# One transformer layer on one core: attention values as two scaled fp16 halves, a fixed instruction order, and weight splits on GpSimd

## The chip, the cores and the metric

The kernel runs on 1 core of one Trainium2 chip, as one launch. The core has a matrix engine (TensorE, called PE in the profile, with its weight loads PEld), three elementwise engines (VectorE or DVE, ScalarE or ACT, GpSimd or POOL) and a queue engine (SyncE or SP) that here issues nearly all DMAs. Each engine works through its own list of instructions in order and waits at an instruction whose operands are not ready. The metric is the device time in microseconds (us), the median of the runs shown. PE works in its fp32 replacement type (fp32r, shown as f32 or fp32r), so products that must be exact to fp32 are made of three: high half by high half, and the two crossed ones.

## The reference, cut to what matters

One layer maps 1024 latent tokens (width 1024) and 256 context tokens to 1024 latent tokens: a modulated norm, one wide input projection, two mixers side by side (attention and a bidirectional mLSTM), a gated merge, then a gated feed-forward net. The change touches the attention and what is drawn from the same activations `h` beside it:

```python
q = apply_rope(rms_norm(heads(aq, 16, 64), q_norm_w), cos, sin)
k = apply_rope(rms_norm(heads(ak, 4, 64), k_norm_w), cos, sin);  v = heads(av, 4, 64)
# per block of 128 queries: keys of the blocks b-1, b, b+1 with |i-j| <= 128, and all 256 context keys
s = concat(where(valid, q k^T, -1e30), q k_ctx^T) * 64 ** -0.5
p = softmax(concat(s, sink))                    # sink: one learned logit per head
att = p[lat] v + p[ctx] v_ctx                   # 16 query heads share 4 key/value heads
y = (sigmoid(ga) * (att w_branch_att) + sigmoid(gm) * (ml w_branch_ml)) w_out
```

`ga` and `gm` are projections of the same `h`; the kernel computes these two while it is in the attention.

## The kernel before, in words

The program runs in stages: startup (modulation, norms, context projections, and the latent activations turned into `hH`, `hL`, the two halves of `h`), attention, mLSTM, and the tail (merge and feed-forward net). The change leaves the mLSTM and the tail as they are.

**Rounds.** `stage_attention` walks through 4 groups g (one key/value head and its four query heads) of 8 blocks b of 128 tokens: 32 blocks. Round n works on four blocks at once: it projects block n (`proj`, 24 matmuls of 384 columns into `pq`; `projected` then makes norms, rotary products and values), turns block n-1 into key and query layout (`stacks`: transposes `qt`, halves `QT`, `KA`, `KB`), computes the scores of block n-3 for four heads (`scores`), and the weighted values of block n-4 (`pv`). Between these lies `filler`: one tile of `ga` or `gm`, 24 matmuls of 512 columns, 32 tiles in all.

**One head of scores** (`head`, lines 677 to 694): four matmuls into a bank `s` (there are two such banks); a fused DVE pass adds the mask, scales and takes the running extreme (L683); ACT makes the shift (L688), the probabilities as fp16 `P` (L691) and again in fp32 over `s` with their sum (L692); DVE makes the low half, fp32 minus fp16 (L693), and a DMA transpose on SP turns both halves into `T` (L694). `P` has three buffers, `T` two.

**Values.** `V` holds a value head as two fp32r halves. [...] `end` adds the two halves of the result, multiplies by the turned reciprocal sum `R`, which goes through DRAM (`norm_row`), and stores.

**Weights.** Projection and gate weights come as fp32 through a pool of two raw buffers and are split into halves by ACT (the copy, L46) and DVE (the rest, L76 and L51). `mod_product` sums a row of later modulation weights, one or two DVE passes a round over the one buffer `wmb` (L234, L236).

**Order.** The program is written as a recipe; a scheduler lays every engine's list out from it by its own estimates. `issue_after` pins a few instructions behind others.

## Time and profile before

| what | value |
|---|---|
| median of 3 runs | 1930.26 us (1928.48 to 1932.29) |
| the profiled execution, its own time | 1935.92 us |
| its span, first to last instruction | 1934.1 us |
| PE busy in the span | 1847.9 us |
| DVE, ACT, POOL busy | 1446.8, 1031.2, 432.2 us |
| first attention projection on PE | 102.5 us |
| first score matmul | 130.7 us |
| first mLSTM matmul | 667.9 us |

The profile is of one execution. Times are microseconds from the first instruction. A group row names the line of the kernel, the engine, the operation, what it writes and reads, its shape and count; then busy time in us and mean duration in ns; then the engine's idle time just before these instructions and what ended it. A timeline row has start, duration, engine, line and tiles; in square brackets stands the idle time before it and what ended that. Matmuls overlap in the pipeline, so what one costs in a stream is the distance between starts, which is shorter than the duration shown.

### The profile page before, as it was taken

What the parts mean: (1) busy time and instruction counts of PE and PEld (TensorE: products, weight loads), DVE (VectorE), ACT (ScalarE), POOL (GpSimd) and SP (SyncE); (2) the same over time, 40 slices, a digit from 0 to 9 for tenths busy, and PEclk for the clock granted to TensorE, in tenths of its full rate; (3) what the DMA queues carried; (4) which work ended last, traced back from release to release, by engine and by line L of the source; (5) the groups of instructions that cost most, each with busy time, mean ns of one, the idle gap of its engine ahead of it and who ended that gap; (6) DMA issues with size and microseconds to landing.
All of it is one profiled execution on the core that took longest, in us unless ns stands there. A gap on an engine that the chain in (4) does not pass through costs nothing.

```text
span 1934.1 us, 27646 instructions
## 1 busy us (share of the span) xinstructions
PE 1847.9 (96%) x9061; PEld 1558.6 (81%) x9061; DVE 1446.8 (75%) x2864; ACT 1031.2 (53%) x2110; POOL 432.2 (22%) x733
## 2 busy tenths in 40 slices
PE   7899889989988899999999999999999999999999
PEld 4877777777777698988888888888888888888887
DVE  3857667878676568586758778769989888897565
ACT  4746666666666645354446556256545444455441
POOL 1225556555545623030211012010000000000000
PEclk9999999999999999999999999999999999999999
DMA  9547667767665942426235982822354544499851
GB/s 359 163 135 169 140 129 156 164 149 178 134 156 113 201 139 82 167 78 223 85 117 186 379 322 87 288 88 78 140 200 181 196 153 176 162 326 346 299 171 66
DMA packets 301984, 342.46 MB, mean 177 GB/s; under 512 B 175872, under 2 KB 200464, under 8 KB 299024
## 3 DMA queue, kind: packets, MB, share of 16 engines
q1 hardware_dynamic: 287440, 314.47, 53.4%
q10 hardware_dynamic: 14400, 26.22, 4.2%
q8 instruction: 72, 1.18, 0.3%
q14 instruction: 72, 0.59, 0.1%
HBM read 224.61 MB, written 76.16 MB: 156 GB/s over the span
## 4 chain that ended last, share of the span: by engine, by line
PE 63%; DVE 10%; DMA 7%; ACT 7%; POOL 7%; issue 5%; ACTq 0%; SPq 0%; POOLq 0%; DVEq 0%
PE pa L1682 4%; PE pa L1684 4%; PE pa L1683 4%; PE g L758 3%; PE yb L1682 2%; PE yb L1683 2%; PE yb L1684 2%; PE dx L1684 2%; PE dx L1682 2%; PE dx L1683 2%; PE pb L1682 2%; PE pb L1684 2%; PE pb L1683 2%; DMA T<-P 2%; ACT s L692 2%
## 5 line engine op out<-in xcount | busy, mean ns | idle before, releaser
L683 DVE CUSTOM_DVE_ANT_0 s<-s,maskA,nsink 128x640 f32<-128x640 f32 (+1 forms) x128 | 115.9, 910 | 30.6 <-PE s L680 30.6
L693 DVE TENSOR_TENSOR P<-s,P 128x640 f16<-128x640 f32 (+1 forms) x128 | 100.7, 787 | 43.9 <-ACT s L692 43.4
L718 POOL CAST ph<-T 128x512 fp32r<-128x512 f16 x152 | 98.6, 649 | 115.8 <-DMA T<-P 73.2
L758 PE MATMUL g<-hH,fh 128*128 128x512 f32 x256 | 105.7, 413 | 4.8 <-ACT fo L46 3.4
L758 PE MATMUL g<-hH,fl 128*128 128x512 f32 x256 | 104.6, 409 | 0.0
L758 PE MATMUL g<-hL,fh 128*128 128x512 f32 x256 | 104.1, 407 | 0.0
L691 ACT ACTIVATE P<-s,st 128x640 f16<-128x640 f32 (+1 forms) x128 | 97.9, 765 | 3.2 <-ACT st L688 0.2
L718 POOL CAST pl<-T 128x512 fp32r<-128x512 f16 x152 | 96.4, 634 | 0.0
L692 ACT ACTIVATE s<-s,st 128x640 f32<-128x640 f32 (+1 forms) x128 | 94.0, 734 | 0.0
L585 PE MATMUL pq<-w1h,hH 128*128 128x384 f32 (+1 forms) x256 | 88.7, 347 | 3.3 <-ACT w1h L46 2.1
L585 PE MATMUL pq<-w1h,hL 128*128 128x384 f32 (+1 forms) x256 | 91.3, 357 | 0.0
L585 PE MATMUL pq<-w1l,hH 128*128 128x384 f32 (+1 forms) x256 | 88.5, 346 | 2.0 <-DVE w1l L76 2.0
L1096 POOL TENSOR_SCALAR kwh<-k,gcall 128x128 fp32r<-128x128 f32 x72 | 33.7, 472 | 232.5 <-PE dC L99 148.2
L677 PE MATMUL s<-KA,QT 128*128 128x384 f32 (+1 forms) x128 | 45.9, 358 | 31.2 <-DVE P L693 13.6
L98 PE MATMUL kv<-w1h,hH 128*128 128x384 f32 x208 | 71.6, 344 | 2.1 <-DVE VL L51 1.9
L1820 ACT ACTIVATE cv<-ua,vecT 128x1024 f32<-128x1024 f32 x22 | 27.4, 1244 | 84.6 <-DVE ua L1793 84.6
L99 PE MATMUL kv<-w1l,hH 128*128 128x384 f32 x208 | 70.5, 339 | 0.0
L100 PE MATMUL kv<-w1h,hL 128*128 128x384 f32 x208 | 70.3, 338 | 0.0
L1682 PE MATMUL dx<-dwh,dfh 128*128 128x512 f32 (+1 forms) x176 | 68.4, 388 | 0.0
L1684 PE MATMUL dx<-dwh,dfl 128*128 128x512 f32 (+1 forms) x176 | 68.3, 388 | 0.0
L1683 PE MATMUL dx<-dwl,dfh 128*128 128x512 f32 (+1 forms) x176 | 68.2, 387 | 0.0
L46 ACT ACTIVATE dfh<-drf 128x512 fp32r<-128x512 f32 x55 | 34.3, 628 | 58.5 <-PE dx L1683 26.4
(610 smaller groups left out, 6387.8 us busy)
## 6 DMA issues: line engine op xcount, KB each, us to landing
ur<-in_w_up SPq DMA_DIRECT2D x22, 1024.0 KB
wmb<-in_w_modB SPq DMA_DIRECT2D x48, 256.0 KB
f_d<-cv SPq DMA_DIRECT2D x22, 512.0 KB
wm<-in_w_modA SPq DMA_DIRECT2D x16, 512.0 KB
fr<-in_w_g SPq DMA_DIRECT2D x32, 256.0 KB
drf<-fs_d SPq DMA_DIRECT2D x15, 512.0 KB
drw<-wt_d SPq DMA_DIRECT2D x14, 512.0 KB
w1b<-in_w_cx SPq DMA_DIRECT2D x16, 388.0 KB
```

Source lines behind the costliest of these rows:

```text
L98: nc.tensor.matmul(ps, lh[:, ls], rh[:, rs], start=start and i == 0, stop=False)
L99: nc.tensor.matmul(ps, lh[:, ls], rl[:, rs], start=False, stop=False)
L585: return lambda: nc.tensor.matmul(ps[:, :wn], x, w[:, :wn], start=i == 0, stop=i == len(todo) - 1)
L683: nc.vector.tensor_tensor_reduce(e, e, mask, scale=ss[:, h : h + 1], scalar=nsink[:, hh : hh + 1], op0=ALU.add, op1=ALU.min, accum_out=st4 ...
L691: nc.scalar.activation(hi, e, AF.Exp, bias=m, scale=-1.0)
L692: nc.scalar.activation(e, e, AF.Exp, bias=m, scale=-1.0, accum_out=st4[:, 4 + h : 5 + h])
L693: nc.vector.tensor_tensor(lo, e, hi, op=ALU.subtract)
L718: nc.gpsimd.tensor_copy(x, T[:, i * nk + kb].rearrange("p h q -> p (h q)"))
L758: return lambda: nc.tensor.matmul(ps, w, x, start=i == 0, stop=i == len(todo) - 1)
L1682: nc.tensor.matmul(ps, lh, rh, start=start and i == 0, stop=False, skip_group_check=True)
L1683: nc.tensor.matmul(ps, lh, rl, start=False, stop=False, skip_group_check=True)
L1684: nc.tensor.matmul(ps, ll, rh, start=False, stop=stop and i == n - 1, skip_group_check=True)
```

## The change

**Values as fp16.** `V` (latent) and a new `Vx` (context, per group) are kept as two fp16 halves, scaled so that they fit: from the sum of squares of the group's value weights, the modulation and the context values a bound is made (`value_bound` once at startup, `value_squares` and `value_scale` once per group: ACT squares, one matmul by ones, two DVE passes, three small POOL passes), whose root is the factor `down` and whose inverse is `up`. `up` enters where `V` is written, `down` where the reciprocal sums are turned (`norm_row`). `T` then goes into the product as it is: the 304 casts and their buffers are gone, and each of the 304 value matmuls is fp16 by fp16.

**Order.** The loop stands under `manual_schedule`: each engine gets the attention's instructions in the order in which they are written, with every head, transpose, projection and gate piece put at a chosen place. The four blocks per round stay; there are 36 rounds where there were 37, and gate tile 0 is in round 0, tile j in round j+2. The low half of the fourth head, its transpose and the sum move to the start of the next round.

**GpSimd splits** the gate weights and, for groups 1 to 3, the projection weights (`gate_split`, `weight_split`: a cast and a subtraction each), loaded one to three rounds ahead. The query scale goes into the norm weight, so one small POOL pass per block is gone; the key's factor goes into the rotary products, and POOL writes the key twice, so one ACT pass (`kf`) is gone. The modulation rows get two buffers.

Around one block of the third group, PE's list had, before (`g`: gate tile, `s`: scores, `po`: weighted values; `Pool_49` is a wait for POOL):

```order
L758 MATMUL g9_1_4960<-hH4_90,fl9_1_4771 128x512
L722 MATMUL po2_2_4964<-ph2_2_0_4965,V2_3861 128x512 [waits Pool_49]
L722 MATMUL po2_2_4964<-pl2_2_0_4966,V2_3861 128x512 [waits Pool_49]
L722 MATMUL po2_2_4964<-ph2_2_1_4969,V2_3861 128x512 [waits Pool_49]
L722 MATMUL po2_2_4964<-pl2_2_1_4970,V2_3861 128x512 [waits Pool_49]
L677 MATMUL s2_3_3_5101<-KA2_3859,QT2_3_4652 128x384 [waits DVE_49,PE_49]
```

and now:

```order
L736 MATMUL s2_3_2_4794<-KcB_127,QT2_3_4413 128x256
L581 MATMUL g10_0_4780<-hH2_88,fl10_0_4401 128x512
L581 MATMUL g10_0_4780<-hH3_89,fh10_0_4400 128x512
L581 MATMUL g10_0_4780<-hL3_97,fh10_0_4400 128x512
L581 MATMUL g10_0_4780<-hH3_89,fl10_0_4401 128x512
L581 LDWEIGHTS V2_3683 [waits DMAHW7_49,DMAHW4_49,DMAHW2_49]
L581 MATMUL po2_2_4818<-T2_2_4528,V2_3683 128x512 [waits DMAHW0_49]
```

All value matmuls of a block now stand in one piece behind head 2's scores, and the wait for the four transposes (`DMAHW`), which POOL's first cast had, stands in PE's own list.

POOL's list around the same block had, before:

```order
L718 CAST ph2_2_2_4973<-T2_2_4779 128x512 [waits PE_49]
L718 CAST pl2_2_2_4974<-T2_2_4779 128x512 [waits PE_49]
L600 TENSOR_SCALAR ss2_6_5056<-ss2_6_5056 128x5 [waits DVE_49]
L718 CAST ph2_2_3_4977<-T2_2_4779 128x512 [waits PE_49]
L718 CAST pl2_2_3_4978<-T2_2_4779 128x512 [waits PE_49]
L718 CAST ph2_2_4_4981<-T2_2_4779 128x512 [waits PE_49]
L718 CAST pl2_2_4_4982<-T2_2_4779 128x512 [waits PE_49]
L601 TENSOR_TENSOR ss2_6_5056<-ss2_6_5056,expo_62 128x5 [waits Pool_49]
```

and now:

```order
L798 TENSOR_TENSOR o22_1_4664<-o22_1_4664,R17_4636 64x512 [waits DMAHW6_49,DMAHW3_49,DVE_49]
L571 CAST fh11_0_4745<-fr11_0_4698 128x512 [waits DMAHW5_49,PE_49]
L572 TENSOR_TENSOR fl11_0_4746<-fr11_0_4698,fh11_0_4745 128x512 [waits PE_49,Pool_49]
L571 CAST fh11_1_4749<-fr11_1_4700 128x512 [waits DMAHW6_49,PE_49]
L572 TENSOR_TENSOR fl11_1_4750<-fr11_1_4700,fh11_1_4749 128x512 [waits PE_49,Pool_49]
L639 TENSOR_SCALAR ss2_6_4829<-ss2_6_4829 128x5 [waits DVE_49]
L640 TENSOR_TENSOR ss2_6_4829<-ss2_6_4829,expo_62 128x5 [waits Pool_49]
L672 TENSOR_TENSOR qf2_6_4834<-qf2_6_4834,t22_6_4835 128x256 [waits DVE_49]
```

The block's norm factors `ss` and rotary sum `qf` no longer stand among casts that wait for PE to free a buffer; the gate weights' splits stand there instead, two rounds ahead of their use.

At the end of the startup SP's list had, before (`w1r`: first projection weights):

```order
L529 DMA vx_d_105<-kvx2_1_961 128x388 [waits DMAHW3_49,DVE_49]
L221 DMA wmb0_1113<-in_w_modB 128x512 [waits DMAHW4_49,PE_49]
L529 DMA vx_d_105<-kvx3_0_1073 128x372 [waits DMAHW5_49,DVE_49]
L529 DMA vx_d_105<-kvx3_1_1077 128x372 [waits DMAHW6_49,DVE_49]
L73 DMA w1r25_1128<-in_w_att0 128x800 [waits DMAHW7_49,DVE_49]
```

and now:

```order
L855 DMA wr0_1_1134<-in_w_att0 128x800 [waits DMAHW1_49]
L523 DMA vx_d_105<-kvx2_0_973 128x388 [waits DMAHW2_49,DVE_49]
L523 DMA vx_d_105<-kvx2_1_976 128x388 [waits DMAHW3_49,DVE_49]
L855 DMA wr0_2_1140<-in_w_att0 128x800 [waits DMAHW4_49,DVE_49,Activation_49]
L855 DMA wr0_3_1146<-in_w_att0 128x800 [waits DMAHW5_49,DMAHW1_49,DVE_49]
L564 DMA fr0_0_1152<-in_w_g 128x512 [waits DMAHW6_49,DMAHW4_49,DVE_49]
```

The four loads of the first projection weights have moved ahead of the gate's and, the first of them, by some dozen DMAs; before, they stood behind the store of the last context columns (`vx_d<-kvx3`).

The diff, cut to its core (the products, the splits, the scale and the loop):

```diff
-        nc.gpsimd.tensor_scalar(ss[:, :4], ss[:, :4], -(HD ** -0.5), 1.0, op0=ALU.mult, op1=ALU.mult)
-                nc.gpsimd.tensor_copy(x, T[:, i * nk + kb].rearrange("p h q -> p (h q)"))
-                split_from(nc, fh, fl, raw)
...
+    def weight_split(g, k2):
+        raw = RAW.pop(("w", g, k2))
+        h, lo = wts.halves(f"a{g}_{k2}", raw.shape[2])
+        nc.gpsimd.tensor_copy(h, raw)
+        nc.gpsimd.tensor_tensor(lo, raw, h.bitcast(F32), op=ALU.subtract)
...
+                V=kp.tile([P, NB, P], F16, tag="V", name=f"V{g}"),
+                Vx=kp.tile([P, NCB, P], F16, tag="Vx", name=f"Vx{g}"),
...
+    def value_scale(g, ps, q):
+        nc.tensor.matmul(ps[:, 448:453], at.ones, q, start=True, stop=True)
+        t = wp.tile([P, 4], F32, tag="vs", name=f"vs{g}")
+        nc.vector.tensor_reduce(t[:, 0:1], ps[:, 448:452], axis=AX.X, op=ALU.add)
+        nc.vector.scalar_tensor_tensor(t[:, 1:2], t[:, 0:1], at.bound, ps[:, 452:453], op0=ALU.mult, op1=ALU.add)
+        nc.gpsimd.tensor_scalar(t[:, 1:2], t[:, 1:2], 2.0 ** -30, 1e-30, op0=ALU.mult, op1=ALU.add)
+        nc.gpsimd.tensor_tensor(t[:, 2:3], t[:, 1:2], expo[:, 0:1], op=ALU.pow)
+        nc.gpsimd.tensor_tensor(t[:, 3:4], t[:, 1:2], t[:, 2:3], op=ALU.mult)
+        G[g]["up"], G[g]["down"] = t[:, 2:3], t[:, 3:4]
...
+        copy_act(nc, G[g]["V"][:, b, 0:HD], ps[:, 320:384], scale=G[g]["up"])
...
+            V[:, b, HD:P], ps[:, 320:384], G[g]["up"], V[:, b, 0:HD], op0=ALU.mult, op1=ALU.subtract
...
+        todo = [(V[kb], T[:, i * nk + kb].rearrange("p h q -> p (h q)")) for kb in range(nk) for i in range(2)]
...
+    TILES = {0: 0}
+    TILES.update({j + 2: j for j in range(1, 32)})
+    LAST = N + 4
...
+    with tc.manual_schedule():
+        for n in range(LAST):
...
+            if tile_done:
+                gate_act(*tile_done)
+            if prior:
+                prior.sink_exp()
+            if S:
+                S.product(0)
+                S.top(0)
+                S.exps(0)
+            if prior:
+                prior.low(3)
+                prior.total()
+            mod_sum()
+            ps, new = proj(*now) if now else (None, Products())
+            new.some(14)
+            pt = turn(*turned) if turned else (tp_tile(f"nr{n}") if prior else None)
+            if out_done:
+                pv_end(*out_done)
+            if n % 2 == 0 and 1 <= n // 2 < 16:
+                for i in range(2):
+                    gate_split(n // 2, i)
...
+            q = value_squares(g) if fresh else None
+            if S:
+                S.product(1)
+            if turned:
+                turned_act(*turned, pt)
+            if S:
+                S.top(1)
+                S.exps(1)
+                S.low(0)
+            new.some(len(new.todo))
+            if prior:
+                prior.norm_turn(pt[0:4, 384:512])
+            if fresh:
+                value_scale(g, ps, q)
...
+            gate.some(8)
+            if turned:
+                turned_dve(*turned, pt)
...
+            if S:
+                S.product(2)
+            gate.some(4)
+            sq = values_act(*now, ps) if now else None
+            if prior:
+                prior.norm_row(pt[0:4, 384:512])
+            if S:
+                S.top(2)
+                S.exps(2)
+                S.low(1)
...
+            po, old = pv(*valued) if valued else (None, Products())
+            old.some(10)
+            if now:
+                ss = values_dve(*now, ps, sq)
+                qf, t2 = rope_q(*now, ps)
...
+            if S:
+                S.product(3)
+            o2 = pv_act(*valued, po) if valued else None
+            gate.some(24)
...
+            if S:
+                S.top(3)
+                S.exps(3)
+                S.low(2)
+            if now:
+                rope_k(*now, ps, ss, qf, t2)
+            if valued:
+                nc.vector.tensor_tensor(o2, po[0:HD], o2, op=ALU.add)
+            if S:
+                S.sinks()
+            mod_end()
...
+            prior = S
```

More of the change, by code (lines that the diff above doesn't have):

```diff
@@ L618, in projected @@
-        nc.gpsimd.tensor_tensor(qf, qf, t2, op=ALU.add)
-        S1[(g, b)] = (qf, ss)
-    def norm_row(pt):
-        if not SUMS:
-            return
-        sums, j = SUMS.pop()
-        nc.tensor.transpose(pt, sums, ident)
-        row = wp.tile([4, P], F32, tag="row", name=f"row{j}", bufs=1)
-        copy_act(nc, row, pt)
-        nc.sync.dma_start(norm_d[j].rearrange("(h t) -> h t", h=4), row)
-        R[j] = wp.tile([HD, 512], F32, tag="R", name=f"R{j}", bufs=1)
-        nc.sync.dma_start(R[j], norm_d[j : j + 1].to_broadcast([HD, 512]))
@@ L634, in stacks, with turn @@
+    def turn(g, b):
         qf, ss = S1.pop((g, b))
-        kf = wp.tile([P, 2, HD], F32, tag="kf", name=f"kf{n}", bufs=1)
-        copy_act(nc, kf, qf[:, None, 256:320].to_broadcast([P, 2, HD]), scale=ss[:, 4:5])
-        pt = tp_tile(f"qt{n}")
-        for i in range(2):
+        pt = tp_tile(f"qt{g}_{b}")
+        for i in range(3):
             nc.tensor.transpose(pt[:, i * P : (i + 1) * P], qf[:, i * P : (i + 1) * P], ident)
-        nc.tensor.transpose(pt[:, 256:384], kf.rearrange("p r d -> p (r d)"), ident)
@@ L706, in scores, with norm_turn, norm_row, norm_load @@
-        return head, sums
+        def norm_turn(self, pt):
+            nc.tensor.transpose(pt, self.st4[:, 12:16], ident)
+        def norm_row(self, pt):
+            j = self.g * NB + self.b
+            row = wp.tile([4, P], F32, tag="row", name=f"row{j}", bufs=1)
+            copy_act(nc, row, pt, scale=G[self.g]["down"][0:4])
+            nc.sync.dma_start(norm_d[j].rearrange("(h t) -> h t", h=4), row)
+        def norm_load(self):
+            j = self.g * NB + self.b
+            R[(self.g, self.b)] = wp.tile([HD, 512], F32, tag="R", name=f"R{j}", bufs=1)
+            nc.sync.dma_start(R[(self.g, self.b)], norm_d[j : j + 1].to_broadcast([HD, 512]))
@@ L734, in pv @@
[L734 to L752 removed]
+        po = mm_tile(f"po{g}_{b}")
```

472 lines of the change are left out of this document (268 added, 204 removed).

## The prediction

> **What bounds the kernel now.** I read the page's head and engine sums first, then the 40 slices, then the windows view cut at the first score, the last full round and the first mLSTM matmul, with a piece of the mLSTM for comparison. The columns of a window are start:end, length, busy us and count of PE, PEld, DVE, ACT and POOL, granted clock, DMA share, GB/s.
>
> ```profile
> span 1934.1 us, 27646 instructions
> PE 1847.9 (96%) x9061; PEld 1558.6 (81%) x9061; DVE 1446.8 (75%) x2864; ACT 1031.2 (53%) x2110; POOL 432.2 (22%) x733
> PE   7899889989988899999999999999999999999999
> ```
>
> ```profile
> 130.70:600.00 469.30, 426.31 (x2131) 362.43 (x2130) 347.42 (x839) 304.26 (x755) 257.54 (x396) 0.97 0.68 149
> 600.00:669.70 69.70, 56.38 (x250) 45.09 (x249) 43.28 (x94) 45.49 (x106) 36.45 (x57) 0.91 0.73 160
> 1100.00:1500.00 400.00, 398.46 (x1779) 327.54 (x1778) 336.76 (x483) 213.26 (x351) 24.92 (x20) 1.00 0.50 179
> ```
>
> PE's share of 96% is a mean: slices 2 to 13 have gaps, all later ones are full. From 1100 to 1500 PE is busy 398.46 of 400 us; the order of instructions there is not touched, so whatever is won or lost must arise before 669.7 us and arrives whole at the end. The attention's 28 full rounds last 469.3 us, **16.76 us a round**, with 43 us of idle PE. That idle is not all: after it matmuls run at half pace.
>
> ```profile
> 400.17 0.34 PE L585 MATMUL pq<-w1l,hH 128*128 128x384 f32 x1
> 400.34 0.34 PE L585 MATMUL pq<-w1h,hL 128*128 128x384 f32 x1
> ...
> 403.79 0.36 PE L677 MATMUL s<-KA,QT 128*128 128x256 f32 x1 [1.92 <-DVE st L699]
> 403.99 0.28 PE L678 MATMUL s<-KB,QT 128*128 128x256 f32 x1
> 404.11 0.28 PE L679 MATMUL s<-KcA,QT 128*128 128x256 f32 x1
> ...
> 407.21 0.63 PE L758 MATMUL g<-hL,fh 128*128 128x512 f32 x1
> 407.64 0.63 PE L758 MATMUL g<-hH,fl 128*128 128x512 f32 x1
> ...
> 409.77 0.39 PE L758 MATMUL g<-hL,fh 128*128 128x512 f32 x1
> 410.00 0.39 PE L722 MATMUL po<-pl,Vc 128*128 128x512 f32 x1
> ```
>
> From start to start a 384-column matmul takes .173 us, a 256-column one .12, a 512-column one .23, but .43 some microseconds after the 1.92 us wait. A round's need at full pace is 24 × .1735 = 4.16 (projection), 24 × .2315 = 5.55 (gate), 4 × (2 × .174 + 2 × .117) = 2.32 (scores), 10 × .231 = 2.31 (values) and about .55 of transposes: **14.9 us**. The round loses 1.9 us to waits and to slow matmuls behind them. Who makes PE wait:
>
> ```profile
> POOL ph L718 <- DMA T<-P: 65.5, 21, 8.4
> PEld po L722 <- POOL ph L718: 13.2, 21, 2.0
> PE s L677 <- DVE st L699: 11.6, 11, 2.3
> PE s L677 <- DVE P L693: 9.4, 11, 2.4
> ```
>
> Two chains end last: casts on POOL before the value products, and DVE's list, where the pass that frees a score bank stands behind others.
>
> **The change part by part.** POOL, DVE and ACT first (the figure behind the first bar's comma is the mean of one, in ns).
>
> ```profile
> L718 POOL CAST ph<-T 128x512 fp32r<-128x512 f16 x128 | 82.4, 644 | 100.6 <-DMA T<-P 65.5 <-PE po L722 15.0 <-DMA norm_d<-row 5.7
> L728 POOL TENSOR_TENSOR o<-o,R 64x512 f32<-64x512 f32 x26 | 34.5, 1328 | 84.3 <-DVE st L700 49.9 <-DVE o L727 28.2 <-DVE P L693 4.9
> L683 DVE CUSTOM_DVE_ANT_0 s<-s,maskA,nsink 128x640 f32<-128x640 f32 x84 | 78.9, 944 | 17.2 <-PE s L680 17.2
> L693 DVE TENSOR_TENSOR P<-s,P 128x640 f16<-128x640 f32 x83 | 68.1, 821 | 25.9 <-ACT s L692 25.5
> L51 DVE TENSOR_TENSOR fl<-fr,fh 128x512 fp32r<-128x512 f32 x25 | 24.4, 975 | 1.9 <-ACT fh L46 1.9
> L76 DVE TENSOR_TENSOR w1l<-w1r,w1h 128x768 fp32r<-128x768 f32 x12 | 13.5, 1126 | 3.2 <-ACT w1h L46 3.2
> L691 ACT ACTIVATE P<-s,st 128x640 f16<-128x640 f32 x83 | 65.7, 791 | 1.9
> L692 ACT ACTIVATE s<-s,st 128x640 f32<-128x640 f32 x83 | 63.2, 761 | 0.0
> L688 ACT ACTIVATE st<-st,shift 128x1 f32<-128x1 f32 x111 | 32.2, 290 | 38.0 <-DVE st L683 34.5 <-DVE st L700 2.5
> ```
>
> *POOL* is busy 257.54 us in the 28 rounds, 9.2 a round; 164 of it are the casts (128 of each half, .64 each). What stays is 3.3 a round. It gains the splits: half a gate tile by a cast of .64 and a subtraction, which no row shows on POOL (nearest, L728, 1.33; bounds .64 and 2.0): 1.97 a round, and the weight split about 1.2. Its sum is 6.5 to 7.3 of 14.9 us, done rounds ahead of the use: hidden. Only the key's second rotary add, under .5 us, lies in the key's path.
>
> *DVE* is busy 347.42 / 28 = 12.4 us a round, and loses L51 and L76, 1.35 of it. Set end to end for a block with three key blocks, its groups' means make 14.2 a round before and **12.9** now. *ACT* loses the copies behind these splits and `kf` (all L46), 1.3 us: end to end from 12.85 to 11.5. Both now lie two microseconds or more below PE's 14.9.
>
> *The fixed order.* I laid one round by hand from these durations, time 0 at head 0's product on PE. PE comes to head 1 at 3.4, the gate at 5.8, head 2 at 7.7, the values at 9.2, head 3 at 11.5, the end at 14.9. Head 3's low half of the round before ends on DVE at 2.6, so head 1's bank is free .8 us early; head 0's low ends at 5.9 (needed 7.7), head 1's at 10.2 (needed 11.5). The projection's slot comes free .9 us early, when the rotary products have read it; the turn's inputs, two us early. Nothing on this sheet makes PE wait, and the smallest margin is .8 us. But the margins hang on DVE's list of 12.9 us running with little delay, so the full floor is unlikely.
>
> *Values without casts.* The wait for `T` moves into PE's list, ahead of the 10 value matmuls; behind it stand the rest of the gate and head 3's product, and all of DVE's and ACT's work on head 3 waits for that. A transpose after the low half:
>
> ```profile
> 402.97 0.68 DVE L693 TENSOR_TENSOR P<-s,P 128x512 f16<-128x512 f32 x1
> ...
> 407.31 0.61 POOL L718 CAST ph<-T 128x512 fp32r<-128x512 f16 x1 [3.65 <-DMA T<-P]
> ...
> 650.46 4.64 DMA T<-P
> 663.89 2.73 DMA T<-P
> ```
>
> Low half ended 403.65, first reader 407.31: 3.7 us. With low 3 at 2.6 `T` is there at 6.3 and wanted at 9.2: 2.9 us of slack, cost zero; at 4.64 + .8 of issue it still fits. No fp16 matmul stands in the trace; I take the .23 of the fp32r row of the same width, and a tenth either way is 304 × .023 = 7 us, which goes into the range. The Trainium skill, "TensorE: Matmul & The Clock Gate", section "Back-to-back issue gap", gives N/2.4 + 2.5 ns for an isolated gap, 216 ns at 512 columns, and 131 ns in a sustained stream. The row of before has 230 for fp32r; by the page 304 value matmuls would be 4 to 30 us shorter if fp16 runs so and fp32r does not. No run here shows it, so it is left out of the sum.
>
> *Start.* The first weights were loaded behind the stores of context columns.
>
> ```profile
> 93.51 0.60 PE L435 MATMUL xt<-ident,x 128*128 128x128 f32 x4
> 96.19 1.54 SPq L73 DMA_DIRECT2D w1r<-in_w_att  x2
> 102.51 0.45 PE L585 MATMUL pq<-w1h,hH 128*128 128x400 f32 x1 [2.05 <-ACT w1h L46]
> 130.68 0.28 PE L677 MATMUL s<-KA,QT 128*128 128x256 f32 x1
> ```
>
> The four loads, .77 us of issue each, move past a dozen others on SP, the context stores among them; these come 3 us later, and their reader, the first value product, is four rounds away: no cost. Loaded early, the weights are split when `x` is turned at 94. Then projection 4.3 → 98.3, gate tile 0 with the value scale 5.8 → 104.1, second projection 4.3 and a little → 108.8; the third round's turn waits for the norm chain of ACT, DVE and POOL passes, about 6.5 → 115.4; copies → first score at 116, taken as 117 (bounds 114, nothing waits; 122, the POOL chains of the scale are in the way) against 130.7: **−13.7**. Two gate tiles fewer are done by then; they lie in the rounds counted next.
>
> *End.* Before, 69.7 us from 600 to the point where only mLSTM is left. Now one full round, then round 32 (no projection, ACT-bound) 11, round 33 10.5, rounds 34 and 35 together 15: four heads on ACT 9.5, a low half .8, a transpose 2.7, eight value matmuls 1.9. Sum r + 36.5, with ±5 for the bare end.
>
> *The sum* for a round of r us: start −13.7; 28 rounds 28 r − 469.3, less 1 (edge blocks with two key blocks save 6.4, 400-wide projections and three rounds with a new group's scale, estimated at 1.5 each, cost 5.4); end r + 36.5 − 69.7. At the floor, r = 14.9: −85. At today's 16.76: −31. Break-even is r = 17.8. **I take r = 15.2**, near the floor because the sheet has no wait, .3 above it for collisions of DMAs and small delays on DVE: −13.7 − 44.7 − 18.0 = −76.4. The profiled execution takes 1935.92 us, 5.7 above the median; it would be 1859.5, the median 1930.26 − 76.4 = **1854 us**.
>
> **The rivals.** *A: DVE becomes the bound.* DVE passes with two operands in SBUF stretch while POOL works:
>
> ```profile
> 426.66 0.69 DVE L51 TENSOR_TENSOR fl<-fr,fh 128x512 fp32r<-128x512 f32 x1
> 432.61 1.28 POOL L728 TENSOR_TENSOR o<-o,R 64x512 f32<-64x512 f32 x1 [3.82 <-DVE st L700]
> 432.90 1.54 DVE L51 TENSOR_TENSOR fl<-fr,fh 128x512 fp32r<-128x512 f32 x1 [0.28 <-ACT fh L46]
> ```
>
> The same pass takes .69 with no wide POOL pass beside it and 1.54 beside L728, and ends .55 after L728 has ended. POOL's splits can do this to the 1.5 modulation passes a round (both operands in SBUF), each held for nearly a whole split of 1.97, say 1.8 us, in a list with .8 us of margin: DVE 12.9 + 2.7 = 15.6, r = 15.6, −65, about 1865. It decides once the holds add up to 2 us a round. Against it: most DVE passes read a PSUM bank, and POOL works 7.3 us at most where it worked 9.2 before. The Trainium skill, "SBUF — State Buffer", section "Who interferes with whom", calls this one shared port pair, taken as an exclusive lock. The two rows above agree.
>
> *B: the round stays as it is*, because a chain of four heads through PE, DVE, ACT and back to a bank, rather than casts, sets it: r = 16.76, −31, about 1899. For it: bank waits (L699, L693) are as long as the casts'. Against it: the sheet.
>
> *C, slower: PE stands at the value products.* PE has no fill ahead of `T` that it may take out of turn, so if `T` lands more than 6.6 us after low 3 (2.9 of slack over 3.7), the rest of the gate and head 3 are late by the excess, in every round; with slow matmuls after each idle, half as much again. Slower than before needs r above 17.8, 2.6 over forecast: a landing some 9 us after the low half, in nearly all rounds, against 8.4 as the longest single wait for `T` now, in which POOL's own early arrival is counted. At 18.2 it gives +12, about 1942.
>
> **How the numbers follow.** Forecast .62, A .18, B .11, C .06; other cases .03. The range reaches from 1836 (floor of 14.9, first score at 114, the end 5 shorter and a little) to 1890 (into B, r = 16.45); outside remain C, part of B and some of the rest, under .2. Faster than before is everything but C and half the rest; .2%, 3.9 us, is about what a measurement of this kernel tells from none: faster .92, same .02, slower .06.
>
> **What would show it.** Right: the first score at 114 to 122, round starts 15 to 15.5 us apart, next to no PE idle at the value products, a clock of 1.00 in the rounds, no casts of `T`, mLSTM beginning near 593. A shows as full DVE slices and modulation passes above 1.5 us; B as bank waits before score products of a microsecond or more; C as idle on the values' weight load, ended by `T`. The whole is wrong if PE's idle per round is not below .5 us, or if PE's later stages change their length.

## The result and the profile after

The changed kernel takes **1877.4 us** (median of 4 runs, 1875.2 to 1879.1) against 1931.3 (4 runs, 1928.5 to 1934.2): ratio 0.972, 95% interval 0.9702 to 0.9739. That is 54 us, 2.8%, where 76 were forecast. The two profiled executions differ by 58.0 us (1935.92 and 1877.91), since the profiled one of before lay 4.6 us above its median and that of now 0.5. The page's head, engine sums, PE's slices and the granted clock:

```profile
span 1876.1 us, 27488 instructions
PE 1820.5 (97%) x9071; PEld 1526.3 (81%) x9071; DVE 1415.1 (75%) x2828; ACT 1010.6 (54%) x2078; POOL 365.0 (19%) x549
PE   8989999999996999999999999999999999999999
PEclk9999999999997999999999999999999999999999
```

Of the attention's gaps two slices are left: the third (94 to 141 us, the start) and the thirteenth (563 to 610 us, the end). The windows view, cut at the first projection, the first score, the start of the last round with a projection (28 rounds later) and the first mLSTM matmul (columns as in the prediction):

```profile
90.91:116.61 25.70, 22.39 (x109) 19.95 (x108) 16.94 (x40) 9.48 (x27) 15.62 (x23) 0.94 0.47 138
116.61:542.10 425.49, 413.94 (x2208) 345.12 (x2207) 319.23 (x815) 289.94 (x728) 201.03 (x240) 1.00 0.79 168
542.10:610.12 68.02, 50.85 (x228) 36.55 (x228) 45.93 (x100) 41.48 (x97) 15.04 (x40) 0.84 0.83 186
1050.00:1450.00 400.00, 398.49 (x1779) 327.81 (x1778) 334.59 (x478) 208.60 (x340) 24.89 (x20) 1.00 0.49 176
```

The 28 rounds take 425.5 us in place of 469, **15.20 a round** against 15.2 in the sum, at a clock of 1.00 in place of 0.97. The first score is at 116.6 (forecast 117). But the end, from 542.1 to 610.1, takes 68.0 us; the sum had r + 36.5 = 51.7. That term alone is 16.3 us off. What follows the first mLSTM matmul keeps its length (1876.1 - 610.1 = 1266.0, before 1934.1 - 667.9 = 1266.2). The prediction had cut the end of the kernel before at 669.7, 1.8 us behind that matmul; from 600.0 to 667.9 it is 67.9 us, so in this execution the end is not shorter at all.

PE's groups in the 28 rounds (busy us, mean ns, then idle us just before them):

```profile
L581 PE MATMUL g<-hH,fh 128*128 128x512 f32 x224 | 90.8, 405 | 0.0
L581 PE MATMUL po<-T,V 128*128 128x512 f16 x148 | 36.6, 381 | 0.1
L733 PE MATMUL s<-KA,QT 128*128 128x384 f32 x85 | 34.9, 411 | 0.0
L581 PE MATMUL po<-T,Vx 128*128 128x512 f16 x108 | 27.8, 380 | 0.0
L733 PE MATMUL s<-KA,QT 128*128 128x256 f32 x28 | 9.8, 351 | 1.6 <-DVE P L757 1.6
```

Two groups of the kernel before, in its 28 rounds:

```profile
L677 PE MATMUL s<-KA,QT 128*128 128x384 f32 (+1 forms) x113 | 40.1, 355 | 25.9 <-DVE st L699 11.6 <-DVE P L693 9.4 <-DVE st L697 4.8
L758 PE MATMUL g<-hH,fl 128*128 128x512 f32 x201 | 81.6, 406 | 0.0
```

The 25.9 us of idle ahead of a head's first score matmul are now 1.6. The count of the gate's matmuls matters for what follows: 224 of each kind are 28 tiles, one in every round, where the kernel before had 201, 25 tiles, and left three rounds without. So 28 rounds now hold 16.7 us more of gate work (3 x 5.55) in 43.5 us less time. The two tiles more that the kernel before did ahead of its first score, and one at its end, are the other side of this.

A useful measure is therefore **lost time**: the length of the 28 rounds less what PE needs in them (28 x 14.9, less 6.4 for blocks at the edges, less 5.55 for each gate tile that is elsewhere, and less 3.3 where the products are fp16, see the last section).

| kernel | 28 rounds | PE's need | lost |
|---|---|---|---|
| before | 469.0 | 394.2 | 75 |
| fp16 values alone, old order | 426.8 | 390.9 | 36 |
| fixed order alone | 497.9 | 407.5 | 90 |
| fixed order, POOL splits, copies of T on POOL | 483.1 | 407.5 | 76 |
| fixed order, fp16 values, ACT and DVE split | 467.8 | 407.5 | 60 |
| the change | 425.5 | 407.5 | 18 |
| the change, one split moved | 419.5 | 407.5 | 12 |

Each row is one profiled execution. The change and the three experiments that leave these rounds as they are (6, 7 and 10) took 424.2 to 428.1 us, so a difference of four us in this table tells nothing.

### The profile page after: what moved, and what is told of

Read it like the earlier page. It is cut to its first block, busy times and chain, and to the rows that moved or that the text cites. A ratio compares the mean times of both kernels' runs of the same rounds, so it can differ in the third digit from the quotient of the medians.

```text
span 1876.1 us, 27488 instructions
## 1 busy us (share of the span) xinstructions
PE 1820.5 (97%) x9071; PEld 1526.3 (81%) x9071; DVE 1415.1 (75%) x2828; ACT 1010.6 (54%) x2078; POOL 365.0 (19%) x549
## 4 chain that ended last, share of the span: by engine, by line
PE 81%; DVE 7%; DMA 5%; ACT 3%; issue 2%; POOL 2%; SPq 0%; POOLq 0%; ACTq 0%; DVEq 0%
PE g L581 9%; PE pq L581 6%; PE pa L1846 4%; PE pa L1848 4%; PE pa L1847 4%; PE po L581 3%; PE yb L1848 2%; PE yb L1846 2%; PE yb L1847 2%; PE dx L1848 2%; PE dx L1846 2%; PE dx L1847 2%; PE pb L1846 2%; PE pb L1848 2%; PE pb L1847 2%
## 5 line engine op out<-in xcount | busy, mean ns | idle before, releaser
L749 ACT ACTIVATE st<-st,shift 128x1 f32<-128x1 f32 x128 | 37.6, 294 | 121.3 <-DVE st L741 121.3
L581 PE MATMUL pq<-w1ha,hH 128*128 128x384 f32 (+1 forms) x256 | 88.0, 344 | 6.9 <-DVE t L661 6.9
L581 PE MATMUL pq<-w1ha,hL 128*128 128x384 f32 (+1 forms) x256 | 87.8, 343 | 0.0
L581 PE MATMUL pq<-w1la,hH 128*128 128x384 f32 (+1 forms) x256 | 87.6, 342 | 0.0
L46 ACT ACTIVATE dfh<-drf 128x512 fp32r<-128x512 f32 x55 | 34.4, 628 | 58.3 <-PE dy L1847 23.6
L51 DVE TENSOR_TENSOR dfl<-drf,dfh 128x512 fp32r<-128x512 f32 x55 | 37.7, 688 | 35.0 <-ACT dfh L46 35.0
L733 PE MATMUL s<-KA,QT 128*128 128x384 f32 (+1 forms) x128 | 51.5, 403 | 8.2 <-DVE P L757 4.6
```

The costliest lines, as they stand in the source:

```text
L581: nc.tensor.matmul(self.ps, x, w, start=self.i == 0, stop=self.i == self.n - 1)
L733: nc.tensor.matmul(s[:, self.lat], q, G[g]["KA"][:, ks], start=True, stop=False)
```

## The experiments

Each ratio is to the kernel before, run on the same chip.

**1. The fp16 values alone.** In the kernel before, `V` and the context's `Vc` become fp16 (unscaled: the factors are left out) and POOL's casts of `T` to fp32r (`ph` and `pl`) go:

```diff
-            ph = pp.tile([P, 512], F32R, tag="ph", ...)
-                nc.gpsimd.tensor_copy(x, T[:, i * nk + kb].rearrange("p h q -> p (h q)"))
+            parts.append([T[:, i * nk + kb].rearrange("p h q -> p (h q)") for i in range(2)])
```

> The kernel before with one part of the change alone: the values as fp16 halves, so that the transposed probabilities enter the products as they are and the 304 casts are gone. The order is the old one, the splits stay on ACT and DVE, and the factors up and down are left out (unscaled halves). If the casts were what held the rounds (theory 1: the waits of PE for POOL, 13.2 + 9.0 + 4.8 us in the 28 rounds, with slow matmuls behind them), it takes 1890 to 1905 us, 25 to 40 less than before, most of the change. If the order of the lists is the cause (theory 2), the waits move to T and to the score banks and it takes 1915 to 1932. I expect about 1905.

Measured: 1896.8 us, ratio 0.9822 (0.9804 to 0.9841). The same two windows, and two groups of PE in the first:

```profile
130.28:557.08 426.80, 402.72 (x2130) 325.95 (x2128) 343.73 (x840) 306.55 (x759) 107.37 (x141) 1.00 0.71 164
557.08:627.82 70.74, 51.56 (x254) 37.25 (x252) 47.38 (x101) 43.66 (x104) 11.79 (x33) 0.91 0.89 206
...
L718 PE MATMUL po<-T,V 128*128 128x512 f16 x148 | 40.4, 382 | 4.6 <-issue 1.9 <-DMA T<-P 1.6 <-ACT w1h L46 1.1
L677 PE MATMUL s<-KA,QT 128*128 128x384 f32 x85 | 34.9, 411 | 11.0 <-DVE P L693 4.8 <-DVE st L699 4.2 <-DVE st L697 1.7
```

34 us (1931.0 to 1896.8) come from this part alone, with the order still left to the scheduler, which laid the lists out anew. Most of it is not the wait at the value matmuls: PE's idle time in the 28 rounds falls from 43.0 to 24.1 us, above all at the score banks (25.9 to about 11 us), and its busy time by 23.6 us, mostly since the clock comes back from 0.97 to 1.00. The casts were the cause, as theory 1 says, but they acted mostly through the lists behind them.

**2, 3, 4. The fixed order without its partners.** In the changed kernel, copies of `T` on POOL go back ahead of every value matmul (fp16 to fp16, one placement of several that are possible), or the splits go back to ACT and DVE, or both:

```diff
+                    nc.gpsimd.tensor_copy(x, T[:, i * nk + kb].rearrange("p h q -> p (h q)"))
...
-        nc.gpsimd.tensor_copy(h, raw)
-        nc.gpsimd.tensor_tensor(lo, raw, h.bitcast(F32), op=ALU.subtract)
+        split_from(nc, h, lo, raw)
```

Both (the order alone):

> The changed kernel with its fixed order, but with the casts and the splits where they were: POOL copies each 128x512 piece of T (fp16 to fp16, which fits the memory; the products stay fp16), PE's value matmuls wait for these copies one by one with a gate matmul between, and ACT and DVE split the weights. Theory 1 (casts): a round cannot be shorter than before, 16.5 to 17 us, 1905 to 1930 in all. Theory 2 (order): rounds of 15 to 15.5 us, 1880 to 1895. POOL then has 4 us of its own and 6.4 of copies in a round of 14.8, DVE 14.2, ACT 12.8, so no engine is full; I expect 1895.

The copies alone:

> The changed kernel with only the copies of T put back on POOL (fp16 to fp16, ten a round, one ahead of each value matmul); the weight splits stay on POOL too. POOL has 7.3 + 6.4 = 13.7 us in a round of 14.8, and the norm factors and the rotary adds stand behind the copies. If POOL's load matters (theory 1), PE's projection slot comes free late and the round is 16 us or more, 1910 or above. If a fixed order hides it (theory 2), 1880 to 1885. I expect 1910.

The splits alone:

> The changed kernel with the weight splits back on ACT (the copy) and DVE (the rest), in the same places of the order; the products stay as changed. DVE then has 14.2 us of a round of 14.8 and ACT 12.8. If the sheet of the prediction is right, whose smallest margin on DVE's list was .8 us, a split of about 1 us on DVE eats it in two rounds of three: .3 to 1 us a round, 1885 to 1905. If PE alone sets the round, no change against the changed kernel, 1875 to 1880. If DVE is held by POOL's two-operand passes in the changed kernel (rival A), taking them away from POOL makes it faster or equal. I expect 1890.

Measured: 1959.8 us (ratio 1.0149, 1.0134 to 1.0164), 1940.4 (1.0046, 1.0031 to 1.0061) and 1919.1 (0.9941, 0.9922 to 0.9961). All three are far above what I expected; the first two are **slower than before**, by 1.5% and 0.5%. A copy takes as long as the cast did, and PE waits for it (the copies' group and the wait, of the run with copies alone):

```profile
L795 POOL COPY ph<-T 128x512 f16<-128x512 f16 x256 | 148.7, 622 | 49.5 <-DMA T<-P 19.8 <-PE po L796 15.4 <-PE qt L772 8.6
PE po L796 <- POOL ph L795: 41.4, 27, 6.7
```

With the splits back, one place shows how a list in a fixed order passes a late load on. The rows of ACT, DVE and PE of that run, in one round:

```profile
198.41 0.84 ACT L46 ACTIVATE w1ha<-wr 128x768 fp32r<-128x768 f32 x1 [4.56 <-DMA wr<-in_w_att]
199.28 0.96 DVE L51 TENSOR_TENSOR w1la<-wr,w1ha 128x768 fp32r<-128x768 f32 x1 [4.45 <-ACT w1ha L46]
201.99 0.66 PE L731 MATMUL s<-KA,QT 128*128 128x384 f32 x1 [5.89 <-DVE P L755]
```

ACT stands at a copy whose weights have not come, DVE at the rest of the split, and the low half that frees a score bank is queued behind it: PE loses 5.9 us. In the 28 rounds of that run ACT waits 30.6 us for weights (18.6 for the projection's, 12.0 for the gate's). On POOL the same split has no head's work behind it. So moving the splits to POOL, at these places of the order, is worth 42 us (1919.1 to 1877.4), which the prediction's sum had only as relief for DVE and ACT. With the copies placed like this the order by itself loses time against the scheduler's (90 us lost against 75). Even with the fp16 values it does: experiment 4 takes 22 us more than experiment 1 (1919.1 against 1896.8, on the same chip), and both leave the splits on ACT and DVE (experiment 4 also makes the factors and loads the first weights early). The order gains only with both partners. Splits on POOL in the scheduler's order were not run, so what they would bring without the fixed order is open.

**5, 6. The early loads of the first weights.** To the kernel of experiment 1 the loads are added where the change has them; and in the changed kernel they are put back behind the last context store:

```diff
+    W0 = wts.load(A["w_att0"], 400)
```
```diff
+        with tc.issue_after(E.vxs.ins):
+            nc.sync.dma_start(raw, A["w_att0"][:, 2 * k2 : 2 * k2 + 2, :])
```

> The kernel of the first experiment (old order, fp16 values, no scale, splits on ACT and DVE; 1896.8 us) with one more edit: the four loads of the first projection weights stand where the changed kernel has them, ahead of the last context stores. If the start's gain (first score at 116.6 us in place of 130.7) comes from these loads, it follows here without any fixed order: first score at 116 to 119, 1882 to 1885 us. If it comes from the fixed order, the first score stays near 130 and the time near 1896. I expect 1883.

> The changed kernel with only these four loads put back behind the last store of context columns. Loads as the cause: the first score 10 to 14 us later, 1888 to 1892 us. Fixed order as the cause: 1877 to 1880. I expect 1890.

Measured: 1897.8 us (0.9833, 0.9817 to 0.9848) and 1889.4 (0.9793, 0.9776 to 0.9810). The second is as expected, the first is a miss: nothing gained over experiment 1, and the first score at 124.9 us, where 116 to 119 were expected. PE's rows say why. Experiment 1, then 5, then 6:

```profile
95.92 0.50 PE L754 MATMUL g<-hH,fh 128*128 128x512 f32 x1 [1.39 <-ACT fh L46]
101.43 0.45 PE L585 MATMUL pq<-w1h,hH 128*128 128x400 f32 x1 [0.56 <-ACT w1h L46]
```
```profile
92.78 0.43 PE L587 MATMUL pq<-w1h,hH 128*128 128x400 f32 x1
97.35 0.50 PE L756 MATMUL g<-hH,fh 128*128 128x512 f32 x1
...
624.26 1.86 PE L720 MATMUL po<-T,Vc 128*128 128x512 f16 x4 [11.28 <-DMA T<-P]
```
```profile
99.85 0.70 PE L581 MATMUL pq<-w1ha,hH 128*128 128x400 f32 x1 [7.76 <-ACT w1ha L46]
```

In the old order a gate tile filled the time in which the weights came, at a cost of 1.39 + 0.56 us of idle. There was little to win: the first score came 5.4 us earlier (130.3 to 124.9), and the end took 4.9 more (70.7 to 75.6 us), where the last `T` was waited for 11.3 us. In the fixed order the projection comes first, and late weights leave PE idle for 7.8 us. The early loads are a condition of this order, not a gain of 13.7 over the old kernel.

**7. More work in the end.** Rounds 32 to 34 get a projection that nobody reads:

```diff
+            if not now and n < LAST - 1:
+                new = proj(NKV - 1, n - N + 1)[1]
```

> The changed kernel with work added: 24 projection matmuls, whose sums nobody reads, in each of rounds 32, 33 and 34, where the projection has run out (72 matmuls, 12.5 us at full pace). The end of the attention, from the last full round's start to the first mLSTM matmul, took 68.0 us against 51.7 in the sum. If PE's waits and the slow matmuls behind them made it long (theory 1), the added work fills the waits, the granted clock in rounds 32 to 34 rises from .8 towards 1, and the end is no longer than before, perhaps some us shorter: 1872 to 1878. If ACT and DVE set the length whatever PE does (theory 2), the clock rises too and the time stays within 1 us, 1876 to 1879. If PE's work adds up (theory 3), 1885 to 1890. I expect 1876.

Measured: 1885.4 us (0.9765, 0.9744 to 0.9787), 8 more than the change: theory 3's band, by the time alone. By the windows of the profiled execution the end itself grew by less:

```profile
121.80:549.88 428.08, 415.93 (x2208) 346.81 (x2206) 319.48 (x815) 290.54 (x728) 200.55 (x241) 0.99 0.79 167
549.88:619.67 69.79, 56.90 (x300) 45.70 (x300) 46.51 (x101) 41.70 (x97) 13.92 (x40) 0.92 0.80 170
```

The end takes 69.8 us with 12.5 us more work. In the change it took 68.0, but two other kernels whose end is the changed kernel's (experiments 6 and 8) took less:

```profile
556.16:621.14 64.98, 49.02 (x228) 35.75 (x227) 45.20 (x99) 41.60 (x97) 15.03 (x40) 0.87 0.87 192
543.32:607.69 64.37, 47.77 (x228) 34.50 (x227) 45.88 (x99) 41.41 (x97) 14.13 (x40) 0.90 0.86 198
```

So the added 12.5 us cost 1.8 to 5.4 in the end. Of the 10.0 us by which this profiled span is longer than the change's, 5.2 lie ahead of the first score and 2.6 in the 28 rounds, where the two kernels are alike. Why the time rose by 8 is not settled by this run. That PE's work alone does not set the end's length is supported, and experiment 9 supports it again.

**8. No factors.** `up` and `down` are 1, the squares and the scale are left out:

```diff
-            q = value_squares(g) if fresh else None
+            if fresh:
+                G[g]["up"] = G[g]["down"] = at.ones[:, 0:1]
```

> The changed kernel without the factors of the values: no sums of squares, no bound, no root; up and down are 1 (the halves are unscaled). Three rounds in which a new group starts take 18.3 to 19.5 us against 14.8 of the others, and the start has 1.5 us of PE waiting for the squares. If the squares on ACT, ahead of the turned keys' copies, make these rounds long (theory 1), they come down to 16 to 17 us and the time is 1868 to 1872. If POOL's splits of two weight pieces, ahead of the norm factors, do it (theory 2), they stay above 17.5 and the time is 1874 to 1877. I expect 1872.

Measured: 1871.0 us (0.9695, 0.9676 to 0.9715); this interval overlaps the change's. The time fits theory 1, the rounds do not: those of groups 1 to 3 take 16.8, 19.0 and 19.9 us, where the change has 18.3, 19.5 and 19.2. Only the first is clearly shorter, and the 28 rounds take 425.0 us against 425.5. The profiled span is 6.7 us shorter through its end (3.7) and the stages behind the attention (4.3), which the edit leaves alone, so the agreement of the time with theory 1 is not evidence for it. In the second POOL and then PE still wait (rows of this run):

```profile
312.30 0.82 POOL L557 CAST w1ha<-wr 128x768 fp32r<-128x768 f32 x1 [3.98 <-DMA wr<-in_w_att]
317.25 0.44 PE L581 MATMUL pq<-w1ha,hH 128*128 128x384 f32 x1 [2.31 <-DVE t L661]
```

**9, 10, 11. The end and the rounds where a group starts.** Three edits of the changed kernel: gate tiles move out of rounds 8, 16 and 24 into rounds 2, 34 and 35; two of the next stage's loads are held, until the attention's last copy of values and its last transpose; and, with both of these, the squares stand later on ACT:

```diff
-    TILES.update({j + 2: j for j in range(1, 32)})
+    TILES.update(zip([r for r in range(2, 36) if r % 8 or r > 24], range(1, 32)))
```
```diff
+                with tc.issue_after(E.pvlast.ins):
+                    nc.scalar.dma_start(o, src)
...
+        wts.late = E.tlast if h == 0 else None
         w = wts.load(A["w_mlqo"][h], 384)
```

> The changed kernel with the gate tiles dealt out otherwise: none in rounds 8, 16 and 24, where a new group starts and where a round took 18.3 to 19.5 us; tile 1 in round 2, and tiles 30 and 31 in rounds 34 and 35, where PE had nothing but scores and value products. The weight splits follow. The same work in all. From the run with 72 added matmuls in the tail, which cost 1.8 us there for 12.5 us of work (theory: PE has idle time in the tail that other work may have), the two tiles in the tail cost 1 to 3 us, the start 2 to 4, and the three rounds become 14 to 16 us, 9 to 12 less: 1868 to 1873 us. Rival: the rounds in which a group starts are set by waits, not by PE, and stay above 17: 1877 to 1882. I expect 1870.

> The changed kernel with the next stage held back: the loads of the branch sums (in_w_ba, with their four DVE passes) and of the mLSTM's query weights (in_w_mlqo, with their splits on ACT and DVE) start only behind the last transpose of the attention. If this work of the next stage, standing between the last heads' passes on DVE and ACT and on the DMA queues, is what made the end 68 us against 51.7 (theory 1), the last round falls from 23.5 us to about 19 and round 32 from 16.5 to about 14: 1869 to 1873, unless the mLSTM then waits for its weights. If the heads' own chain sets it (theory 2), the end stays at 66 to 68 us, 1875 to 1879. I expect 1873.

> The two edits before this together, and a third: the squares of the value weights on ACT stand behind the keys' and queries' copies, and the factor is made behind head 2's product, so that neither is ahead of what PE waits for. In the run without factors the three rounds with a new group kept 16.8 to 19.9 us, so I give the third edit 1 us in each. If the gains add: 1870 + 1873 - 1877 - 3 = 1863 us; if they overlap (the same idle time of PE filled twice), 1867 to 1870.

Measured: 1876.4 us (0.9727, 0.9711 to 0.9743), 1875.2 (0.9726, 0.9711 to 0.9740) and 1885.7 (0.9773, 0.9758 to 0.9787): no difference from the change, no difference, and slower by half a per cent, where 1870, 1873 and 1863 to 1870 were expected. The windows of the end, of experiments 9 and 10:

```profile
544.32:610.96 66.64, 56.83 (x277) 42.91 (x275) 42.77 (x95) 41.97 (x98) 16.36 (x44) 0.97 0.86 190
547.30:611.61 64.31, 49.60 (x229) 35.78 (x228) 41.62 (x95) 40.92 (x96) 13.11 (x40) 0.86 0.75 158
```

Two more gate tiles (11 us of work) leave the end at 66.6 us, with the clock at 0.97 in place of 0.84: PE's pace does not seem to be its bound either. Holding the next stage back gives 64.3, but experiments 6 and 8, whose end is the changed kernel's, had 65.0 and 64.4: no effect on the whole can be told. And rounds 8, 16 and 24, with 5.55 us less work for PE, came down only to 17.4, 16.2 and 16.0, with 16.4 to 17.6 in the round behind: they are set by a wait, not by PE's work. Experiment 11 made them 16.7, 20.2 and 22.1; that the later factor did this is likely but not tried apart.

**12. The split that waits.** In the changed kernel POOL's list has the fourth piece of a new group's weights ahead of the norm factors `ss` of the block before. POOL's rows, and what PE then waits for:

```profile
311.89 0.82 POOL L557 CAST w1ha<-wr 128x768 fp32r<-128x768 f32 x1 [4.08 <-DMA wr<-in_w_att]
312.79 1.81 POOL L558 TENSOR_TENSOR w1la<-wr,w1ha 128x768 fp32r<-128x768 f32 x1
314.97 1.17 POOL L640 TENSOR_TENSOR ss<-ss,expo 128x5 f32<-128x5 f32 x1
316.83 0.44 PE L581 MATMUL pq<-w1ha,hH 128*128 128x384 f32 x1 [2.59 <-DVE t L661]
```

The split is moved to the start of the round that uses it, behind `ss` and the rotary adds, and that round's gate split one round on (with the held loads of experiment 10):

```diff
                 weight_split(n // 8 + 1, 2)
-                weight_split(n // 8 + 1, 3)
...
+            if fresh and g:
+                weight_split(g, 3)
             ps, new = proj(*now) if now else (None, Products())
```

> The run with the next stage held back, and one more edit: the split of the fourth piece of a new group's projection weights stands behind the norm factors and rotary adds of the block before it (at the start of the round that uses it, in place of the round before), and the gate split of that round is one round later. In the changed kernel POOL waited 2.8 and 4.1 us for the load of this piece with the norm factors queued behind, and PE then 1.7, 2.6 and 2.6 us for its projection slot. If this wait is what makes the three rounds long, they come down from 18.3, 19.5 and 19.2 us to 15.5 to 17 and the time from 1875.2 to 1866 to 1870. If something else in these rounds (the squares, the scale, DMA) makes them long whatever POOL does, they stay above 17.5 and the time is 1873 to 1877. I expect 1868.

Measured: 1868.3 us (1866.8 to 1876.2), ratio 0.9707 (0.9688 to 0.9726). The three rounds:

```profile
191.06:207.31 16.25, 15.13 (x82) 12.42 (x81) 13.30 (x31) 12.20 (x36) 8.66 (x14) 1.00 0.79 148
310.97:327.26 16.29, 15.20 (x82) 12.49 (x82) 12.03 (x31) 11.38 (x34) 7.83 (x13) 1.00 0.55 123
430.44:446.70 16.26, 15.12 (x81) 12.42 (x80) 13.29 (x31) 12.20 (x36) 8.64 (x14) 1.00 0.66 146
```

16.3 us each, 8.2 less in all than in the change and 8.5 less than in experiment 10, from which this run differs by the moved splits alone. POOL no longer waits for this load and PE no longer at the projection, so the split standing ahead of `ss`, and its wait for the load, was the cause. The gate split that moved with it stood behind `ss` already. The 28 rounds take 419.5 us, below the 424.2 to 428.1 of the kernels that leave them alone. The ratio of 0.9707 lies below the 0.972 of the change and the 0.9726 of experiment 10, but the intervals overlap, so the kernels' times do not tell them apart for sure; the rounds do. It beats the kernel before.

## Why the prediction was right, and where not

*The number.* 1877.4 us lies inside the range, but 23 above the forecast, and closer to the 1865 of rival A than to it; only the rows tell them apart. Some 5 of the 23 us come from the profiled execution of before, on which the sum was built and which lay above its median; 18.4 lie in the sum's terms. Of the signs named, the first score, the clock of 1.00, the missing casts and PE's idle time (0.41 us a round, under 0.5) came; round starts 15 to 15.5 us apart (14.8, and three long ones) and the mLSTM at 593 (610) did not.

*What bounds.* Right: the gain arose in the attention and arrived whole. The two chains were the right ones too: PE stood 1.6 us at a head's first score matmul in the rounds, against 25.9, and 0.1 at the values. That the casts fed the second chain as well (experiment 1) the prediction did not say.

*The start* (-13.7; measured -14.1). The size was right, the reason only in part. The step "The first weights were loaded behind the stores" booked the time up to the first projection at 102.5 as a gain; a gate tile filled it (experiments 1 and 5). The first score is earlier mainly because two gate tiles (11 us) moved behind it, which the sum did count, in the rounds; the early loads let that happen without idle time (experiment 6). That the two numbers agree to 0.4 us is partly luck: three other kernels with the same start (experiments 7, 10 and 12) have the first score at 121.8, 120.4 and 114.8 us.

*The round* (15.2; measured 15.20). Right in its mean, with errors that cancel, so this agreement is luck in part. A usual round takes 14.8 us, not 15.2, and PE is busy in all of it. The window of four such rounds, and of the longest of the three in which a group starts:

```profile
132.20:191.48 59.28, 59.28 (x313) 49.55 (x313) 45.95 (x114) 40.59 (x99) 29.90 (x31) 1.00 0.87 190
313.41:332.90 19.49, 16.90 (x83) 14.12 (x82) 13.50 (x35) 11.39 (x34) 13.50 (x20) 0.91 0.61 140
```

These three were put at 1.5 us extra each; they take 3.5 to 4.7 more than 14.8. The term was mis-sized because the sheet had only the usual round: POOL's splits were taken as "done rounds ahead of the use: hidden", and the fourth piece, loaded in the very round in which POOL splits it, was not (experiment 12).

*POOL, DVE, ACT.* 1.35 us a round given back to DVE and 1.3 to ACT cost 42 us (experiment 4). 25 of the 42 lie in the six rounds 7, 8, 15, 16, 23 and 24, around the start of a group, where ACT waits longest for weights; the other 22 rounds lost 0.8 us each. That fits the small margin of 0.8 us; the larger cost is a late load with a head's work queued behind it. Weighing the splits' move by busy time alone ("Both now lie two microseconds or more below PE's 14.9") missed that.

*The end* (r + 36.5 = 51.7; measured 68.0) is the step that failed, and it makes nearly all of the miss: by the profiled executions 58.0 us in place of 76.4, 18.4 less, 16.3 of it here and 1.6 more through the cut at 669.7. In experiments 6 and 8, with the same end, it is 65.0 and 64.4, so the term was 13 to 16 us too small. Round 32 was put at 11 us "ACT-bound", 33 at 10.5, 34 and 35 at 15. They took:

```profile
556.83:573.31 16.48, 13.69 (x56) 10.34 (x55) 11.50 (x25) 10.93 (x25) 1.96 (x3) 0.79 0.75 180
573.31:586.60 13.29, 11.41 (x60) 8.64 (x59) 8.30 (x17) 9.67 (x24) 1.80 (x2) 1.00 0.80 148
586.60:610.12 23.52, 11.02 (x38) 5.43 (x38) 11.47 (x26) 8.00 (x22) 7.32 (x32) 0.67 0.80 180
```

ACT is busy 10.9 of 16.5 us: it is not full either. Without the projection PE reaches head 1 as soon as head 0 is done, and the bank is not free; then it waits for a copy that ACT has behind head 0's exponentials, and at the very end for the sum and the last transpose. The last row is DVE's, just ahead of the last low half:

```profile
559.53 0.41 PE L733 MATMUL s<-KA,QT 128*128 128x384 f32 x1 [1.48 <-DVE P L757]
561.67 0.37 PE L772 MATMUL qt<-ident,st 128*4 128x128 f32 x1 [1.31 <-ACT KA L46]
...
604.63 0.37 PE L772 MATMUL nr<-ident,st 128*4 128x128 f32 x1 [5.91 <-DVE st L769]
607.12 1.86 PE L581 MATMUL po<-T,Vx 128*128 128x512 f16 x4 [2.12 <-DMA T<-P]
...
601.47 1.64 DVE L1376 TENSOR_TENSOR s_ba<-s_ba 128x512 f32<-128x512 f32 x1
```

Shown: neither PE's work (experiments 7, 9) nor its clock (9) by itself sets the end. The work of the next stage is a small part of it: this pass on `s_ba` belongs to that stage, and the last low half starts behind it, at 603.03. With it held back (experiment 10) PE waits 3.8 us for the last sum in place of 5.9, but then 3.2 for `T` in place of 2.1: about one us is won. What is left is the heads' chain through four engines in a fixed order, with no projection to fill its waits. That is the chain of rival B; I did not try to shorten it, and the cause stays open as far as that.

*The rivals.* A (DVE held by POOL) did not come as a bound. The modulation pass on DVE, before and now:

```profile
L236 DVE SCALAR_TENSOR_TENSOR macc<-wmb,sil,macc 128x512 f32<-128x512 f32 x36 | 29.2, 812 | 8.2 <-DMA wmb<-in_w_modB 8.2
```
```profile
L837 DVE SCALAR_TENSOR_TENSOR macc<-wmb,sil,macc 128x512 f32<-128x512 f32 x34 | 27.0, 794 | 0.0
```

Its mean fell from 812 to 794 ns. The holds themselves do occur: one of the 34 passes took 1.78 us, beside a gate split on POOL, and the 1.64 us above stand beside POOL's product of `o` and `R` (0.68 for a like pass just before). B had the right worry, since the waits for banks were a second chain; more than half of them went with the casts (25.9 to about 11 us, experiment 1), the rest with the order and the splits. C did not come: the value matmuls waited 0.1 us in the rounds, and 2.1 us for the last block's `T`. (C's +12 at 18.2 us a round is +10.6 by the prediction's own sum; nothing rests on it.)

*What the prediction left out* is the split of the gain. The fp16 values alone bring 34 us, and the order with the POOL splits 19 more; the parts do not add, since the order alone loses 29.

## What to carry to other kernels

Take work off an engine before you fix its order: the same order was 29 us slower than the scheduler's with copies and splits left in, still 22 us slower with the splits alone left in, and 19 us faster than the fp16 values in the scheduler's order once the splits were on POOL. Before a wait ahead of the first use is booked as a gain, look whether another instruction of the list already fills it. Lay out the rounds that differ (a new group, the last ones) by hand too, and for each load ask what stands behind its first reader on that engine; the sheet of the usual round (14.9) was right to 0.1 us and the others held nearly all of the error.

## What the hardware showed

The value matmuls ran faster in fp16 than in fp32r. Ten of them in a round of the change:

```profile
204.22 1.47 PE L581 MATMUL po<-T,V 128*128 128x512 f16 x6
205.53 1.03 PE L581 MATMUL po<-T,Vx 128*128 128x512 f16 x4
```

From the first start of the six to the first of the four are 1.31 us, **0.218 each**, against 0.231 for fp32r in the sum. Over the 256 of the 28 rounds that is 3.3 us, and 4 over all 304, the low end of the prediction's 4 to 30. The Trainium skill's "TensorE: Matmul & The Clock Gate", section "Back-to-back issue gap", gives 216 ns for an isolated gap at this width and 131 in a sustained stream; the trace agrees with the first for fp16, though these ten follow one another, and with neither for fp32r. A POOL copy of 128x512 from fp16 to fp16 (experiment 3) takes 622 ns, hardly less than the cast to fp32r with 644.
